# Query sums of squares in a dilated-attention layer: three plain float32 products on three strips of columns in place of six products of split squares

## The chip, the cores and the metric

The kernel runs on one core of a Trainium2 chip. The metric is the device time of one execution in microseconds (us); the median of the runs is compared. The profile comes from one execution of its own.

## The reference, as far as it matters

A two-layer decoder trunk over 512 tokens of width 1024: layer 0 is a gated DeltaNet mixer and a SwiGLU feed-forward, layer 1 is dilated sliding-window attention and a SwiGLU feed-forward. The change lies in the attention of layer 1. It has three groups of eight heads with 64 features each; every head's queries and keys are RMS-normalised before the scores:

```python
def _rmsnorm(x, w):
    y = x * lax.rsqrt(jnp.mean(x * x, axis=-1, keepdims=True) + RMS_EPS)
    return y * w
...
qkv = (h @ w_in).reshape(b, s, 3, N_DIL_GROUPS, DIL_HEADS_PER_GROUP, DIL_HEAD_DIM)
q = _rmsnorm(qkv[:, :, 0], q_norm)
k = _rmsnorm(qkv[:, :, 1], k_norm)
```

The change concerns the sum of x * x over the 64 features of a query head, for all heads and tokens.

## The kernel before, in words

Activations lie with features on the 128 partitions and the 512 tokens in the columns of a tile. A matrix product with weights is made of three products of halves: every operand is split into a rounded part and a remainder (type float32r), and high x high, high x low and low x high are summed in a PSUM bank (`gemm_steps`, line 431, product at line 441). ScalarE (ACT) rounds a weight block, VectorE (DVE) or GpSimd (POOL) subtracts to get the remainder. SyncE (SP) loads the weight blocks in the order of use (`stream`).

The order of the instructions of each engine is written when the program is built, by a planner (`Weave`): generators stand for jobs, `W.now` is the planned time of TensorE (PE), the wrapped engines `V` (DVE), `S` (ACT) and `G` (POOL) carry planned busy times, and a `yield` of an engine, an event or a pool (`Banks`) parks a generator until the planned time has come. On the chip each engine runs its instructions in that order and waits on semaphores.

In the attention layer (`dilated`, line 1075) a tile of 128 features holds two heads, so each of the three groups g has four pairs p. The main loop runs the jobs of `DJOBS` (line 37): `q21` is the query tile of group 2, pair 1, `k12` the key tile of group 1, pair 2, `u` and `v` jobs make values. Each q or k job is 24 products of 512 columns. The work behind it:

- `q_post` (line 1136): ACT scales the bank into the query tile, and `squares` (line 1125) takes the squares out of the bank on ACT, rounds them with a second pass of ACT and subtracts on POOL. Then the bank and one page go back and the query is announced.
- `k_post` (line 1146): the same squares for a key tile, two products with a block matrix `bones` (lines 1156 and 1157), and a chain on ACT and DVE that scales the key tile itself. It is not changed but for the name of its operand.
- `factors` (line 1246), once for each pair p, when its three queries are there: six products (line 1256) with 6 columns of `bones` each put the sums of three groups x two heads into partitions 0 to 5 of one bank, each group's high and low squares added up. ACT copies the 6 x 512 sums, four turns (`turn`, line 1265) bring the tokens to the partitions, and a chain of small DVE operations makes the scale of the queries (`rq`) and the slopes (`sd`), without which the scores of the pair can't be masked.
- `near`, `far` and `value` (lines 1320, 1373, 1421) make scores, exponentials and outputs of a pair. Scores are plain float32 products (`mat`, line 422) of 64 partitions, the two heads one after the other in the code.

`mat` counts max(2n, n + m) x 0.833 ns of PE for n columns, 0.853 us for 512. Pages are buffers of 128 x 512 floats, 59 of them, of which the planner gives the attention's jobs 30 (`pages`); a q job asks for four, a k job for five (line 1240). `dconst` (line 1060) loads the constants and rounds `bones` during the first feed-forward layer. In the first layer a blocked triangular solve (`merge`) uses plain products of 32x32 on strips of the array; in its second step three products run over each block, the first and the third from partitions 0 to 31 into partitions 32 to 63 and 0 to 31 of the bank, the second from 64 to 95 into 64 to 95.

Of the kernel before, what the change touches and what calls it, by code (L numbers as in the profile page):

```python
# [12 lines left out]
F32R = mybir.dt.float32r  # L13
I32 = mybir.dt.int32
AF = mybir.ActivationFunctionType
OP = mybir.AluOpType
# [6 lines left out]
NCH = T // 128  # L23
# [149 lines left out]
class Trunk:  # L173
# [248 lines left out]
    def mat(self, out, lhsT, rhs, start=True, stop=True):  # L422
        self.nc.tensor.matmul(out, lhsT=lhsT, rhs=rhs, start=start, stop=stop)  # L423
        n, m = math.prod(rhs.shape[1:]), lhsT.shape[-1]
        self.weave.now += max(2 * n, n + m) * 0.833e-3

    def turn(self, out, in_, ident=None):
        self.nc.tensor.transpose(out, in_, self.ident if ident is None else ident)  # L428
        self.weave.now += 0.107
# [630 lines left out]
    def dconst(self):  # L1060

        nc, V = self.nc, self.V
        late = self.ctx.enter_context(self.tc.tile_pool(name="late", bufs=1))
        tile = lambda n, name, dtype=F32: late.tile([128, n], dtype, name=name)
        dc = tile(512 + 96 + 146 + 2 + 36, "dc")
        nc.sync.dma_start(dc, self.a["dconsts"])
        dist = [dc[:, 0:256], dc[:, 256:384], dc[:, 384:512]]
        slopes = lambda p: dc[:, 512 + p * 24:512 + (p + 1) * 24].rearrange("p (g c h) -> p g c h", g=3, c=NCH)
        bones, wqk, eps = tile(146, "bones", F32R), tile(1, "wqk"), tile(1, "eps")
        V.tensor_copy(bones, dc[:, 608:754])  # L1070
        V.scalar_tensor_tensor(wqk, dc[:, 754:755], -0.0625, dc[:, 755:756], op0=OP.mult, op1=OP.mult)
        V.memset(eps, EPS)
        self.dc = dist, slopes, bones, wqk, eps, dc[:, 756:788], dc[:, 788:792]

    def dilated(self):

# [2 lines left out]
        mat, turn = self.mat, self.turn  # L1079
        W, V, S, G, sm, chain, main = self.weave, self.V, self.S, self.G, self.sm, self.ch, self.main  # L1080
        AX = mybir.AxisListType.X
        HB = NCH * 2
        ch = lambda c: slice(c * 128, (c + 1) * 128)
        seg = lambda t: t.rearrange("p (r n) -> p r n", r=4)
        mixed = lambda t, g: t if g else t.rearrange("p (r b n) -> p b r n", b=4, r=4)
        plain = lambda t, g: t if g else t.rearrange("p (b r n) -> p b r n", b=4, r=4)
        with tc.tile_pool(name="ak", bufs=1) as ak, tc.tile_pool(name="aw", bufs=2) as aw:
            dist, slopes, bones, wqk, eps, place, block = self.dc
            half = lambda h: slice(h * 64, (h + 1) * 64)
            fac = lambda i: rr[:, i].rearrange("p (g c) -> p g c", g=3)[:, :, :, None].to_broadcast([128, 3, NCH, 2])  # L1090
            rr = ak.tile([128, 3, 12], F32, name="rr")
# [20 lines left out]
            pages, scores, spaces, both = Banks(W, APAGES), Banks(W, SCORES), Banks(W, VALUES), Banks(W, 1)  # L1112
            qT, kT, vs, qs, rq, sd, om, pt, os_, done, gm = ({} for _ in range(11))
# [8 lines left out]
                done[key] = done.get(key, 0) + 1  # L1122
                return done[key] == n

            def squares(x, out=lambda t: t):

                sq, sh, sl = self.page(), self.page(F32R), self.page(F32R)
                S.activation(out(sq), x, AF.Square)
                yield S
                S.activation(sh, sq, AF.Copy)  # L1130
                yield S
                G.tensor_sub(sl, sq, sh.bitcast(F32))
                yield G
                return sq, sh, sl

            def q_post(g, p, ps):
                q = self.page()
                S.activation(plain(q, g), mixed(ps, g), AF.Copy, scale=wqk)
                sq, sh, sl = yield from squares(mixed(ps, g), lambda t: plain(t, g))
                main.release(0.0)  # L1140
                pages.release(0.0)
                qT[g, p] = q
                qs[g, p] = sh, sl
                W.fire(("q", g, p), G)

            def k_post(g, p, ps):
                t = self.page()
                yield "rb", 2
                V.tensor_mul(plain(t, g), mixed(ps, g), mixed(self.rb, g))
                main.release(V)  # L1150
                yield V
                sq, sh, sl = yield from squares(t)
                y = self.page()
                yield sm
                pn = self.bank()
                self.nc.tensor.matmul(pn, lhsT=bones[:, :128], rhs=sh, start=True, stop=False)
                self.nc.tensor.matmul(pn, lhsT=bones[:, :128], rhs=sl, start=False, stop=True)
                W.now += 0.427
                pages.release(0.0)
                pages.release(0.0)  # L1160
                S.activation(y, pn, AF.Ln, bias=eps)
                S.activation(y, y, AF.Exp, scale=-0.5)
                S.activation(sq, y, AF.Square)
                yield S
                V.scalar_tensor_tensor(sq, pn, EPS, sq, op0=OP.add, op1=OP.mult)
                sm.release(V)
                yield V
                V.scalar_tensor_tensor(y, sq, -3.0, y, op0=OP.add, op1=OP.mult)
                yield V
                pages.release(0.0)  # L1170
                V.tensor_mul(t, t, y)
                pages.release(V)
                kT[g, p] = t
                W.fire(("k", g, p), V)
# [62 lines left out]
            def job(names):  # L1237
                posts = []
                for j in names:
                    post, n = {"q": (q_post, 4), "k": (k_post, 5)}[j[0]]  # L1240
                    for _ in range(n):
                        yield pages
                    posts.append(lambda ps, f=post, g=int(j[1]), p=int(j[2]): f(g, p, ps))
                yield from self.together(posts, 2)

            def factors(p):


                yield ("orders",)
                for g in range(3):  # L1250
                    yield "q", g, p
                yield sm
                t = self.bank()
                for g in range(3):
                    for i, s in enumerate(qs[g, p]):
                        self.nc.tensor.matmul(t[:6], lhsT=bones[:, 128 + g * 6:134 + g * 6], rhs=s,  # L1256
                                              start=g + i == 0, stop=g + i == 3)
                        W.now += 0.2134
                        pages.release(0.0)
                yield pages  # L1260
                sums = self.page()[:6]
                S.activation(sums, t[:6], AF.Copy)
                yield S
                for c in range(NCH):
                    turn(t[:, c * 6:c * 6 + 6], sums[:, ch(c)], self.ident[:6, :6])
                pages.release(0.0)
                x = aw.tile([128, 3, NCH, 2], F32, name="fx", bufs=3)
                y = aw.tile([128, 3, NCH, 2], F32, name="fy", bufs=3)
                f = lambda t: t.rearrange("p g c h -> p (g c h)")
                V.tensor_mul(x, t[:, :24].rearrange("p (c g h) -> p g c h", c=NCH, g=3), fac(1))  # L1270
                sm.release(V)
                yield V
                V.tensor_scalar(f(x), f(x), EPS, None, op0=OP.add)
                yield V
                yield from self.rsqrt(f(y), f(x), aw)
                yield V
                V.tensor_mul(x, x, y)
                rq[p] = aw.tile([128, 3, NCH, 2], F32, name="rq", bufs=4)
                V.tensor_mul(rq[p], y, fac(0))
                yield V  # L1280
                V.tensor_mul(x, x, fac(2))
                yield V
                sd[p] = aw.tile([128, 3, NCH, 2], F32, name="sd", bufs=4)
                V.tensor_mul(sd[p], x, slopes(p))
                W.fire(("rq", p), V)
# [343 lines left out]
def layout(i):  # L1629
    i = {k: np.asarray(v) for k, v in i.items()}  # L1630
    a = {}
    x = i["x"][0]
# [24 lines left out]
    p = np.arange(128)  # L1657
# [7 lines left out]
    q = p % 32 * 4 + p // 32  # L1665
    d = q[:, None] - q[None, :]
    d0 = np.concatenate([np.where(d <= 0, d + 128, far), np.where(d >= 0, d, far)], axis=1)
    d = p[:, None] - p[None, :]
    d1 = np.where(d >= 0, 4 * d, far)
# [2 lines left out]
    slopes = [np.broadcast_to(-(2.0 ** (-8.0 * (head(pair) + 1) / 24)), (3, NCH, 2)).reshape(-1) for pair in range(4)]  # L1672
    slopes = np.broadcast_to(np.concatenate(slopes), (128, 96))
    same = (p[:, None] // 64 == p[None, :] // 64) / 64.0
    which = [np.where(np.arange(6) // 2 == g, p[:, None] // 64 == np.arange(6) % 2, 0) for g in range(3)]
    table = np.concatenate([d0, d1, d2, slopes, same] + which, axis=1).astype(np.float32)
    place = p[:, None] % 32 == np.arange(32)[None, :]
    block = p[:, None] // 32 == np.arange(4)[None, :]
    places = np.concatenate([place, block], axis=1).astype(np.float32)
# [18 lines left out]
```

## Time and profile before

| | us |
|---|---|
| median of 3 runs | 1392.67 |
| lowest and highest run | 1391.41, 1393.38 |
| profiled execution | 1394.09 |
| its span, first to last instruction | 1392.3 |

The profile's engines: PE is matmul, PEld the weight load that overlaps it, DVE VectorE, ACT ScalarE, POOL GpSimd. Idle time of an engine that is not the bottleneck costs nothing. Nearly all vector and scalar instructions carry line 83, that of the wrapper; they are told apart by tile names (`page`, `bank`, `wl`, `pp`, `fx`). A plain float32 product shows as two matmul records, a product of halves as one.

### The profile page before, as it was taken

How to read it: one execution, taken by the hardware profiler on the slowest of the kernel's cores; microseconds unless marked ns; L12 is line 12 of the kernel's file. 1: busy time of each engine (PE TensorE's matmuls, PEld its weight loads, DVE VectorE, ACT ScalarE, POOL GpSimd, SP SyncE). 2: the span in 40 equal slices, each digit the busy share in tenths (PEclk: the TensorE clock that was granted, in tenths of full speed). 3: DMA queues.
4: the chain of work that ended last, by engine and by line, in shares of the span. 5: the costliest groups of instructions: out<-in, count | busy, mean ns of one | idle time of the engine just before them, and what ended most of it. 6: DMA issues, size and time to landing. Idle time of an engine off the chain costs nothing.

```text
span 1392.3 us, 18305 instructions
## 1 busy us (share of the span) xinstructions
PE 1358.0 (98%) x7040; PEld 1121.7 (81%) x7040; DVE 811.9 (58%) x1476; ACT 591.9 (43%) x1268; POOL 265.8 (19%) x234
## 2 busy tenths in 40 slices
PE   8899989999999999999999999999989999999998
PEld 5688878878888888888888888889768888888887
DVE  7888766777555455434437456897675555554222
ACT  4654556863333333322246444665533333332221
POOL 5533800124111111111212111100141111110000
PEclk9999999999999999999999999999999999999999
DMA  4224240134233333333232332111123332333331
GB/s 161 63 74 121 76 119 20 31 122 127 82 101 96 95 102 91 99 98 96 86 91 91 93 90 63 60 46 47 39 67 107 92 105 91 95 103 104 110 107 57
DMA packets 48328, 122.52 MB, mean 88 GB/s; under 512 B 16624, under 2 KB 17008, under 8 KB 48240
## 3 DMA queue, kind: packets, MB, share of 16 engines
q1 hardware_dynamic: 47952, 121.21, 29.0%
q8 instruction: 55, 0.90, 0.3%
q14 instruction: 33, 0.27, 0.1%
q10 hardware_dynamic: 288, 0.14, 0.0%
HBM read 117.66 MB, written 3.67 MB: 87 GB/s over the span
## 4 chain that ended last, share of the span: by engine, by line
PE 84%; DVE 7%; ACT 3%; POOL 3%; issue 2%; DMA 1%; SPq 0%; DVEq 0%; ACTq 0%; POOLq 0%
PE bank L441 71%; PE bank L423 7%; DVE page L83 4%; PE bank L1192 3%; PE bank L428 2%; POOL xblk L83 2%; POOL tblk L83 1%; ACT page L83 1%; DVE wl L83 1%; ACT pp L83 1%; DMA wraw<-in_w 0%; ACT wh L83 0%; PE bank L1256 0%; DVE rsqrt L83 0%; DVE pp L83 0%
## 5 line engine op out<-in xcount | busy, mean ns | idle before, releaser
L441 PE MATMUL bank<-page,wh 128*128 128x512 f32 x2912 | 950.6, 395 | 9.3 <-DVE page L83 4.6
L441 PEld LDWEIGHTS bank<-page,wh 128*128 128x128 f32 x2912 | 550.0, 190 | 128.6 <-DVE page L83 6.5
L441 PE MATMUL bank<-page,wl 128*128 128x512 f32 x1632 | 645.1, 395 | 2.5 <-DVE wl L83 2.4
L83 ACT ACTIVATE wh<-wraw 128x512 fp32r<-128x512 f32 (+1 forms) x432 | 256.3, 616 | 468.6 <-PE bank L441 261.2
L83 DVE TENSOR_TENSOR wl<-wraw,wh 128x512 fp32r<-128x512 f32 (+1 forms) x408 | 341.3, 856 | 162.3 <-ACT wh L83 161.9
L441 PEld LDWEIGHTS bank<-page,wl 128*128 128x128 f32 x1632 | 309.4, 190 | 67.3 <-DVE wl L83 5.2
L83 POOL TENSOR_TENSOR page<-page 128x512 f32<-128x512 f32 (+2 forms) x122 | 179.0, 1470 | 923.0 <-DVE page L83 559.4
L83 DVE TENSOR_TENSOR page<-bank,page 128x512 f32<-128x512 f32 (+1 forms) x123 | 84.7, 690 | 228.8 <-PE bank L441 216.9
L83 ACT ACTIVATE page<-page 128x512 f32<-128x512 f32 (+2 forms) x224 | 140.4, 629 | 123.1 <-POOL page L83 65.9
L441 PE MATMUL bank<-hl,wh 128*128 128x512 f32 x352 | 139.0, 395 | 0.0
L441 PEld LDWEIGHTS bank<-hl,wh 128*128 128x128 f32 x352 | 66.1, 188 | 14.0
L83 DVE TENSOR_TENSOR page<-page,bank 128x512 f32<-128x512 f32 x40 | 27.4, 686 | 71.1 <-PE bank L441 63.9
L83 ACT ACTIVATE pp<-pp,om,rq 128x128 f32<-128x128 f32 (+1 forms) x96 | 43.1, 509 | 13.4 <-DVE om L83 13.2
L1192 PE MATMUL bank<-wh,page 128*128 128x256 f32 x256 | 48.3, 288 | 0.0
L83 DVE SCALAR_TENSOR_TENSOR page<-bank,cp,page 128x511 f32<-128x511 f32 (+2 forms) x63 | 46.7, 742 | 1.6 <-ACT page L83 1.0
L83 DVE SCALAR_TENSOR_TENSOR page<-page,cp 128x512 fp32r<-128x512 f32 (+3 forms) x39 | 45.0, 1166 | 3.7 <-ACT page L83 3.7
L83 DVE SCALAR_TENSOR_TENSOR page<-page 128x512 f32<-128x512 f32 (+1 forms) x52 | 41.8, 804 | 1.1 <-ACT page L83 0.3
L83 POOL TENSOR_TENSOR wl<-wraw,wh 128x512 fp32r<-128x512 f32 x24 | 33.2, 1388 | 45.4 <-ACT wh L83 45.3
L1192 PEld LDWEIGHTS bank<-wh,page 128*128 128x128 f32 x256 | 39.9, 191 | 1.8 <-issue 1.0
L83 ACT ACTIVATE page<-bank 128x512 f32<-128x512 f32 (+4 forms) x37 | 21.0, 568 | 42.1 <-PE bank L423 28.7
L83 DVE SCALAR_TENSOR_TENSOR pp<-dc,sd,bank 128x128 f32<-128x128 f32 (+1 forms) x96 | 33.5, 372 | 8.5 <-PE bank L423 8.5
L1192 PE MATMUL bank<-wl,page 128*128 128x256 f32 x128 | 36.4, 284 | 1.0 <-DVE wl L83 0.9
(174 smaller groups left out, 916.6 us busy)
## 6 DMA issues: line engine op xcount, KB each, us to landing
wraw<-in_fin SPq DMA_DIRECT2D x88, 512.0 KB, 3.6
wraw<-in_w SPq DMA_DIRECT2D x32, 512.0 KB, 3.6
wraw<-in_fout SPq DMA_DIRECT2D x32, 448.0 KB, 3.3
wraw<-in_dqk SPq DMA_DIRECT2D x24, 512.0 KB, 3.6
wraw<-in_fout SPq DMA_DIRECT2D x16, 512.0 KB, 3.6
wraw<-in_w0o SPq DMA_DIRECT2D x8, 512.0 KB, 3.6
wraw<-in_dv SPq DMA_DIRECT2D x8, 512.0 KB, 3.6
page<-in_x SPq DMA_DIRECT2D x8, 256.0 KB, 6.6
```

The source lines that it names most:

```text
L83: return f(out, *args, **kw)
L423: self.nc.tensor.matmul(out, lhsT=lhsT, rhs=rhs, start=start, stop=stop)
L428: self.nc.tensor.transpose(out, in_, self.ident if ident is None else ident)
L441: self.nc.tensor.matmul(ps, lhsT=lhsT[:, c], rhs=rhs, start=k + i == 0, stop=k == len(xs) - 1 and i == 2)
L1192: self.nc.tensor.matmul(ps[c], lhsT=x[:, ch(c)], rhs=w[:, k * 256:(k + 1) * 256], start=b + k + t == 0, stop=b == 1 and k == 3 and t == 2)
```

## The change

The squares of the queries are no longer split. For each pair, three plain float32 products, one for each group, with one 128 x 32 matrix `which` (columns 0 and 1 pick the two heads, the others are zero) write partitions 0 to 31, 32 to 63 and 64 to 95 of one bank. The planner counts the three as one. The copy takes 96 partitions, the turns 96 x 96 of the identity, and the sums are read from two of every 32 columns. `bones` keeps its 128 columns for the keys; `which` stays unrounded in the constants.

```diff
@@ dconst @@
-        dc = tile(512 + 96 + 146 + 2 + 36, "dc")
+        dc = tile(512 + 96 + 160 + 2 + 36, "dc")
...
-        bones, wqk, eps = tile(146, "bones", F32R), tile(1, "wqk"), tile(1, "eps")
-        V.tensor_copy(bones, dc[:, 608:754])
+        bones, wqk, eps = tile(128, "bones", F32R), tile(1, "wqk"), tile(1, "eps")
+        V.tensor_copy(bones, dc[:, 608:736])
...
-        self.dc = dist, slopes, bones, wqk, eps, dc[:, 756:788], dc[:, 788:792]
+        self.dc = dist, slopes, bones, dc[:, 736:768], wqk, eps, dc[:, 770:802], dc[:, 802:806]
@@ q_post @@
-                sq, sh, sl = yield from squares(mixed(ps, g), lambda t: plain(t, g))
-                main.release(0.0)
-                pages.release(0.0)
+                qs[g, p] = self.page()
+                S.activation(plain(qs[g, p], g), mixed(ps, g), AF.Square)
+                main.release(S)
                 qT[g, p] = q
-                qs[g, p] = sh, sl
-                W.fire(("q", g, p), G)
+                W.fire(("q", g, p), S)
+                yield S
@@ job @@
-                    post, n = {"q": (q_post, 4), "k": (k_post, 5)}[j[0]]
+                    post, n = {"q": (q_post, 2), "k": (k_post, 5)}[j[0]]
@@ factors @@
                 for g in range(3):
-                    for i, s in enumerate(qs[g, p]):
-                        self.nc.tensor.matmul(t[:6], lhsT=bones[:, 128 + g * 6:134 + g * 6], rhs=s,
-                                              start=g + i == 0, stop=g + i == 3)
-                        W.now += 0.2134
-                        pages.release(0.0)
+                    mat(t[g * 32:g * 32 + 32], which, qs[g, p])
+                    pages.release(0.0)
+                W.now -= 2 * 0.853
                 yield pages
-                sums = self.page()[:6]
-                S.activation(sums, t[:6], AF.Copy)
+                sums = self.page()[:96]
+                S.activation(sums, t[:96], AF.Copy)
                 yield S
                 for c in range(NCH):
-                    turn(t[:, c * 6:c * 6 + 6], sums[:, ch(c)], self.ident[:6, :6])
+                    turn(t[:, c * 96:c * 96 + 96], sums[:, ch(c)], self.ident[:96, :96])
...
-                V.tensor_mul(x, t[:, :24].rearrange("p (c g h) -> p g c h", c=NCH, g=3), fac(1))
+                V.tensor_mul(x, t[:, :384].rearrange("p (c g h) -> p g c h", c=NCH, g=3)[:, :, :, :2], fac(1))
@@ layout @@
-    which = [np.where(np.arange(6) // 2 == g, p[:, None] // 64 == np.arange(6) % 2, 0) for g in range(3)]
-    table = np.concatenate([d0, d1, d2, slopes, same] + which, axis=1).astype(np.float32)
+    which = p[:, None] // 64 == np.arange(32)
+    table = np.concatenate([d0, d1, d2, slopes, same, which], axis=1).astype(np.float32)
```

## Rows read from the trace of the kernel before

**Rows 1.** The page's head: busy us (share of the span) xinstructions.

```profile
PE 1358.0 (98%) x7040; PEld 1121.7 (81%) x7040; DVE 811.9 (58%) x1476; ACT 591.9 (43%) x1268; POOL 265.8 (19%) x234
```

**Rows 2.** Stretches: us, busy PE, PEld, DVE, ACT, POOL (xinstructions), granted clock, DMA.

```profile
820.00:840.00 20.00, 19.41 (x133) 16.38 (x132) 13.49 (x37) 9.63 (x18) 2.92 (x2) 1.00 0.20 57
...
940.00:960.00 20.00, 18.98 (x164) 18.04 (x164) 17.69 (x47) 15.71 (x35) 0.00 (x0) 1.00 0.14 38
...
980.00:1000.00 20.00, 16.99 (x111) 13.83 (x109) 10.65 (x18) 11.18 (x23) 0.00 (x0) 0.99 0.17 53
1000.00:1006.00 6.00, 6.00 (x14) 4.40 (x15) 3.51 (x6) 3.10 (x5) 2.92 (x3) 0.50 0.00 0
...
1028.00:1034.00 6.00, 6.00 (x15) 4.69 (x16) 1.11 (x2) 0.00 (x0) 0.00 (x0) 0.53 0.14 55
```

**Rows 3.** The chain that ended last, 755 to 800 us: start, us, piece.

```profile
771.03 1.39 PE bank L1256 x6
...
773.55 0.34 PE bank L428 x4
...
780.99 0.44 PE bank L428 x4
```

**Rows 4.** Groups of ACT and POOL, 700 to 930 us: count | busy us, mean ns | idle before.

```profile
L83 ACT ACTIVATE page<-page 128x512 fp32r<-128x512 f32 x25 | 15.5, 624 | 0.3
...
L83 POOL TENSOR_TENSOR page<-page 128x512 fp32r<-128x512 f32 x24 | 32.2, 1343 | 177.4 <-ACT page L83 156.8 <-issue 10.9 <-DVE page L83 6.8
```

**Rows 5.** Timeline of PE around the scores at 864 us: start, us, instruction.

```profile
864.04 0.39 PE L441 MATMUL bank<-page,wl 128*128 128x512 f32 x1
864.27 0.39 PE L441 MATMUL bank<-page,wh 128*128 128x512 f32 x1
864.59 1.16 PE L423 MATMUL bank<-page 64*128 64x128 f32 x16
865.68 0.50 PE L441 MATMUL bank<-page,wh 128*128 128x512 f32 x1
```

**Rows 6.** The chain that ended last, end of the attention stage.

```profile
964.43 5.94 PE bank L423 x54
...
981.38 1.54 ACT pp L83 x4
```

**Rows 7.** Timeline of PE in the first layer's solve, second step.

```profile
192.88 0.19 PE L423 MATMUL bank<-MX,xblk 32*32 32x32 f32 x1
192.88 0.20 PE L423 MATMUL bank<-xblk,MX 32*32 32x32 f32 x2
192.91 0.19 PE L423 MATMUL bank<-MX,xblk 32*32 32x32 f32 x1
192.91 0.20 PE L423 MATMUL bank<-xblk,MX 32*32 32x32 f32 x2
```

**Rows 8.** Timeline of all engines before the first scores, 823 to 827 us.

```profile
823.23 0.69 DVE L83 SCALAR_TENSOR_TENSOR page<-page 128x512 f32<-128x512 f32 x1
...
824.58 1.29 POOL L83 TENSOR_TENSOR page<-page 128x512 fp32r<-128x512 f32 x1 [6.18 <-ACT page L83]
824.62 1.79 DVE L83 TENSOR_TENSOR page<-page 128x512 f32<-128x512 f32 x1
...
826.57 0.38 PE L423 MATMUL bank<-page 64*128 64x128 f32 x2 [0.59 <-DVE page L83]
```

**Rows 9.** Timeline of DVE between 862 and 904 us.

```profile
872.35 0.93 DVE L83 TENSOR_SCALAR fx<-fx 128x24 f32<-128x24 f32 x1
...
874.33 0.16 DVE L83 TENSOR_SCALAR fy<-fx 128x24 int32<-128x24 int32 x1
...
880.14 0.35 DVE L83 SCALAR_TENSOR_TENSOR pp<-dc,sd,bank 128x128 f32<-128x128 f32 x1 [1.81 <-PE bank L423]
```

**Rows 10.** Who waited for whom, PE alone, 700 to 978 us: us in total, times, longest.

```profile
PE bank L1192 <- DVE wl L83: 0.9, 1, 0.9
PE bank L423 <- DVE page L83: 0.7, 2, 0.6
```

More of the change, by code (lines that the diff above doesn't have):

```diff
@@ L1068, in dconst @@
         slopes = lambda p: dc[:, 512 + p * 24:512 + (p + 1) * 24].rearrange("p (g c h) -> p g c h", g=3, c=NCH)
-        bones, wqk, eps = tile(146, "bones", F32R), tile(1, "wqk"), tile(1, "eps")
-        V.tensor_copy(bones, dc[:, 608:754])
-        V.scalar_tensor_tensor(wqk, dc[:, 754:755], -0.0625, dc[:, 755:756], op0=OP.mult, op1=OP.mult)
+        bones, wqk, eps = tile(128, "bones", F32R), tile(1, "wqk"), tile(1, "eps")
+        V.tensor_copy(bones, dc[:, 608:736])
+        V.scalar_tensor_tensor(wqk, dc[:, 768:769], -0.0625, dc[:, 769:770], op0=OP.mult, op1=OP.mult)
         V.memset(eps, EPS)
-        self.dc = dist, slopes, bones, wqk, eps, dc[:, 756:788], dc[:, 788:792]
+        self.dc = dist, slopes, bones, dc[:, 736:768], wqk, eps, dc[:, 770:802], dc[:, 802:806]
     def dilated(self):
@@ L1087, in dilated @@
         with tc.tile_pool(name="ak", bufs=1) as ak, tc.tile_pool(name="aw", bufs=2) as aw:
-            dist, slopes, bones, wqk, eps, place, block = self.dc
+            dist, slopes, bones, which, wqk, eps, place, block = self.dc
             half = lambda h: slice(h * 64, (h + 1) * 64)
@@ L1123, in finished, with squares @@
                 return done[key] == n
-            def squares(x, out=lambda t: t):
+            def squares(x):
                 sq, sh, sl = self.page(), self.page(F32R), self.page(F32R)
-                S.activation(out(sq), x, AF.Square)
+                S.activation(sq, x, AF.Square)
                 yield S
@@ L1155, in k_post @@
                 pn = self.bank()
-                self.nc.tensor.matmul(pn, lhsT=bones[:, :128], rhs=sh, start=True, stop=False)
-                self.nc.tensor.matmul(pn, lhsT=bones[:, :128], rhs=sl, start=False, stop=True)
+                self.nc.tensor.matmul(pn, lhsT=bones, rhs=sh, start=True, stop=False)
+                self.nc.tensor.matmul(pn, lhsT=bones, rhs=sl, start=False, stop=True)
                 W.now += 0.427
```

## The prediction

> **What bounds the kernel now.** I read the page's head first: TensorE (PE) is busy for 98% of the span [rows 1], so a step is worth what it takes from PE's queue, or what it takes from a wait that PE ends on. The table of stretches comes next [rows 2]: in the attention stage the clock is granted whole and PE is full. It idles 0.59 us in 820 to 840, 1.02 us in 940 to 960 and 3.01 us in 980 to 1000; after 1000 come two stretches of 6 us at half clock. VectorE (DVE) is busy 17.69 us of 20 in 940 to 960, so it is the next engine. The chain of waits then tells whether the changed products lie on the path: the six split products of one pair of heads stand on it with 1.39 us, with their four turns behind them [rows 3]. There are four such groups, at 771, 828, 868 and 910 us, all on the chain. Last I read the groups of ScalarE (ACT) and GpSimd (POOL) [rows 4].
>
> A measurement of this kernel can tell about 0.2% from no change, 2.8 us. The profiled execution took 1394.09 us (span 1392.3 us and 1.8 us around it), 1.4 us above the median of 1392.67 us; I sum against 1394.09 and move the difference to the median.
>
> **The products.** Removed: 24 split products, 4 x 1.39 = 5.6 us of PE [rows 3]. Added: 12 plain float32 products with 512 columns. The trace has none of that width. A plain product shows as two records, and one of 128 columns takes 5.94 / 54 = 0.11 us [rows 6]; four times the columns make 0.44 us a record, 0.88 us a product.
>
> Do three run at once? The nearest rows are the 32x32 products of the first layer's solve [rows 7]: three strips, two of them fed from the same rows of the array with different data. Their records come as one and two, one and two, a new triple after 0.03 us, as long as a single record of 32 columns would take by rows 6 (0.11 / 4). So strips of columns that share rows run together, and first halves stand beside first halves. Then a group takes 2 x 0.44 = 0.88 us and what it costs to enter and leave strips. For that I take the scores, two strips of rows [rows 5]: 16 records, eight steps of 0.11 = 0.88 us, and yet 1.09 us pass until the next product starts, 0.21 us of rim; and the product before them holds 0.32 us where its neighbours hold 0.23, another 0.09. The stationary operand here has 32 columns and not 128, so its load should show less. I take 1.10 us a group, between 0.88 (no rim) and 1.18 (all of it). Saved: 0.29 x 4 = 1.2 us. The outer bound is no overlap: 6 x 0.44 + 0.30 = 2.94 us, 1.55 us more a group.
>
> One thing speaks against two steps. If the two records of a product are issued one behind the other and no record overtakes, a strip's second half holds up the next strip's first, and the group is a staircase of four steps, 4 x 0.44 + 0.30 = 2.06 us, 0.67 more than now. The records of rows 7 interleave and show no staircase, so I sum with two steps and keep four as a rival. The Trainium skill (TensorE: Matmul & The Clock Gate, Part 3, "Packing small matmuls") has a rule that would give the staircase: matmuls start and end strictly in program order, without reordering. By it the sum below would be +2.5 us and not -1.4; the trace agrees with it only if the order issued is already the interleaved one, which no row here shows.
>
> **The turns.** Before: four turns of 6 rows in 0.34 us. After: four of 96 rows and 96 columns. The nearest rows are full 128x128 turns, 0.44 us for four [rows 3]; I take that end, +0.10 a group, +0.4 us. The other end is no change. The weighted read of the turned sums has 24 elements as before, and the copy out of the bank has 512 columns as before: nothing.
>
> **ScalarE and GpSimd.** Twelve of the 25 rounding copies go, 12 x 0.624 = 7.5 us of ACT, and twelve of the 24 subtractions, 12 x 1.343 = 16.1 us of POOL [rows 4]. PE's work covers both, and the cover stays: the waits of PE between 700 and 978 us are three on DVE's tiles and weights, none on a bank [rows 10]. So I cost the work itself at nothing, also the earlier return of the query's bank and the two pages fewer.
>
> What it does to DVE counts. At 824.58 POOL subtracts a query's halves (by its place in the order of jobs those of q01), and beside it DVE's product of the key tile takes 1.79 us, where the DVE operations just before it, on as many columns, take 0.69. PE waits 0.59 us for that tile [rows 8]. With the subtraction gone the product ends about 1.1 us earlier, and then PE's own work is late next: -0.6 us. Bounds: 0 (the order shifts and something else is beside it) to -0.6.
>
> The same slowing shows in the busy stretch: 0.93 us at 872 on a tile of 24 columns where the next such operation takes 0.16 [rows 9]. But DVE then waits for PE itself, 1.81 us before 880.14 [rows 9], so this relief is swallowed and I cost it at nothing. The idle time in 940 to 960 is mostly a wait on DVE's split of weights, 0.9 us [rows 10]; little of the relief reaches it. Bounds: 0 to -1.0.
>
> **What moves.** The program's order comes from a planner. It now sees a query ready about one copy and one subtraction earlier (0.62 + 1.34 = 2 us), releases the bank earlier, counts 0.853 us of PE a group where it counted six of 0.2134 = 1.28, and asks for two pages a query, not four. So factors, scores and what follows are placed earlier among the weight products. No DMA is added; SP's queue keeps its order, and the constants' load grows by 14 columns and is issued a whole feed-forward layer earlier. That reordering has no row. I bound it by the waits that stand there: it can remove the 1.02 us of 940 to 960, or add a wait of that kind.
>
> Sum: -1.2 + 0.4 - 0.6 = -1.4 us: 1392.7 for the profiled execution, 1391.3 for the median.
>
> **The rivals.**
> *More waits go.* As forecast, and also the waits in 940 to 960 (-1.0) and half of one stretch at half clock. A product there takes 0.43 us (6 us with 14 records [rows 2]) where it takes 0.23 [rows 5], so a stretch costs 14 x 0.2 = 2.8 us, half of it 1.4. Together -3.8 us, 1388.9. For it: the last pair's factors come 2 us earlier and the tail is a chain of latencies. Against: DVE is nearly full there, and the stretches come after a tail that hangs on the last exponentials [rows 6], whose work does not change.
>
> *The strips don't run together.* The change then doesn't do what it says: +1.55 x 4 + 0.4 - 0.6 = +6.0 us, 1398.7. For it: no row has three strips over all 128 rows with 512 columns. Against: rows 7. It decides from a group of about 2.1 us upward (1.39 + (2.8 + 0.2) / 4).
>
> *Staircase.* The strips overlap by one half only, four steps as worked out above: +0.67 x 4 + 0.4 - 0.6 = +2.5 us, 1395.2. For it: the three products wait for three tiles of their own, and the code issues each product whole. Against: the solve's products are issued whole too, and interleave [rows 7].
>
> *A new wait at the end of the stage.* The order shifts so that scores or values of the last pair stand ahead of something that is not ready; PE is in order, so all weight products behind them wait. One such wait has the size of the 0.9 us on the weights [rows 10], and the time at half clock grows with it by up to a stretch, 2.8 us: -1.4 + 0.9 + 2.8 = +2.3; with two such waits +3.2 us, 1395.9, which I take. It decides beyond 4.2 us of new waits and lost clock (2.8 + 1.4).
>
> **How the numbers follow.** Forecast 0.50, more waits gone 0.23, new wait 0.13, strips apart 0.07, staircase 0.07. Faster by over 0.2%: nearly all of the second case and a little of the first, 0.26. Slower: strips apart, most of the new wait and a little of the staircase, 0.18. Within: 0.56. The forecast's own range is 1390.0 to 1392.3 (below: groups of 0.88 us and turns at nothing, -2.0 - 0.6; above: groups of 1.18 us and the wait at 826 kept, -0.8 + 0.4). The whole range reaches below to a whole stretch at half clock gained beside the waits of the second case (-1.4 - 1.0 - 2.8, 1387.5), above a little beyond the new wait (1396.5), and leaves out the strips apart.
>
> **What would show it.** Three products a pair as six records of about 0.44 us in two steps; from the first of them to the next product's start 1.0 to 1.2 us, and not 2 or 3. Turns of about 0.44 us for four. POOL with 12 subtractions, ACT with 13 rounding copies. The key tile's product before the first scores (near 825 us) at 0.7 us and PE without a wait there. Idle time between 940 and 1000 and the two half-clock stretches as before. The prediction is wrong if the group holds PE for over 1.4 us, or if idle time before 1000 us or time at half clock moves by more than 2 us either way.

## The result, and the profile after

The changed kernel took 1400.47 us (median of 4 runs, 1399.77 to 1402.10) beside 1392.96 us before (4 runs, 1391.41 to 1393.38): 1.0058 times the time, 95% interval 1.0046 to 1.0070, so 7.5 us slower. The prediction said 1391.3 us in a range of 1387.5 to 1396.5: wrong, and on the wrong side. The profiled execution took 1402.1 us with a span of 1400.1; its head on the page, beside [rows 1]:

```profile
span 1400.1 us, 18258 instructions
PE 1360.6 (97%) x7040; PEld 1122.7 (80%) x7040; DVE 805.8 (58%) x1476; ACT 584.7 (42%) x1256; POOL 250.4 (18%) x222
```

POOL has 12 subtractions fewer and ACT 12 rounding copies fewer, but PE is busy for 2.6 us longer. Yet the edited operations are not what costs the time. The timeline of PE at the first group of the changed kernel (start, us, instruction):

```profile
770.60 0.39 PE L441 MATMUL bank<-page,wh 128*128 128x512 f32 x1
770.92 1.06 PE L423 MATMUL bank<-page,dc 128*32 128x512 f32 x6
771.91 0.50 PE L441 MATMUL bank<-page,wh 128*128 128x512 f32 x1
772.24 0.39 PE L441 MATMUL bank<-page,wl 128*128 128x512 f32 x1
...
772.94 0.39 PE L441 MATMUL bank<-page,wl 128*128 128x512 f32 x1
773.17 0.49 PE L428 MATMUL bank<-cc,page 96*128 96x96 f32 x4
773.45 0.71 PE L441 MATMUL bank<-page,wh 128*128 128x512 f32 x2
```

and in the kernel before, behind its group and around its turns:

```profile
772.26 0.39 PE L441 MATMUL bank<-page,wl 128*128 128x512 f32 x1
772.49 0.61 PE L441 MATMUL bank<-page,wh 128*128 128x512 f32 x2
...
773.17 0.39 PE L441 MATMUL bank<-page,wh 128*128 128x512 f32 x1
773.49 0.41 PE L428 MATMUL bank<-cc,page 6*128 6x6 f32 x4
```

From the first record of the group to the next product 0.99 us pass, and the product before holds PE for 0.32 where others hold it for 0.23: 1.08 us where [rows 3] had 1.39. The product behind the group holds 0.33 (771.91 to 772.24), which the kernel before did not have (772.26 to 772.49, 0.23); with it a group costs 1.19 us, 0.2 less than before. The four turns take 0.28 us where they took 0.34, and the product ahead of them holds 0.23 where it held 0.32. So it is in the first and third groups; in the other two, next to scores, the turns take 0.42 and 0.39 us. The groups of ACT and POOL from 700 to 930 us, beside [rows 4]:

```profile
L83 ACT ACTIVATE page<-page 128x512 fp32r<-128x512 f32 x13 | 8.1, 622 | 0.2
...
L83 POOL TENSOR_TENSOR page<-page 128x512 fp32r<-128x512 f32 x12 | 16.3, 1360 | 195.9 <-ACT page L83 190.0 <-issue 5.8
```

The loss stands in two other places. One is the end of the attention stage: who waited for whom, PE alone, 700 to 1020 us (total, times, longest):

```profile
PE bank L441 <- ACT page L83: 5.6, 1, 5.6
PE bank L441 <- DVE page L83: 2.3, 1, 2.3
PE bank L1192 <- DVE wl L83: 0.4, 2, 0.2
PE bank L1192 <- ACT wh L83: 0.4, 1, 0.4
```

In the kernel before, the longest wait of that table was

```profile
PE bank L441 <- ACT page L83: 2.6, 2, 2.3
```

The stretches that answer to [rows 2]:

```profile
820.00:840.00 20.00, 19.41 (x120) 15.36 (x119) 11.86 (x37) 7.80 (x14) 0.99 (x1) 1.00 0.27 80
940.00:960.00 20.00, 19.93 (x172) 18.39 (x170) 16.07 (x44) 15.40 (x36) 0.00 (x0) 1.00 0.16 53
...
980.00:1000.00 20.00, 17.55 (x118) 15.51 (x117) 6.67 (x11) 11.15 (x25) 0.00 (x0) 0.91 0.16 53
1000.00:1020.00 20.00, 14.39 (x51) 11.04 (x50) 14.19 (x17) 7.45 (x12) 7.92 (x6) 0.83 0.09 27
...
600.00:696.00 96.00, 96.00 (x417) 78.03 (x416) 39.22 (x51) 24.97 (x44) 16.61 (x12) 1.00 0.33 96
```

The waits of [rows 10] on a page of 0.6 and on weights of 0.9 us are gone or smaller; but before, the two longest waits up to 1020 us were 2.3 and 0.9 us, now they are 5.6 and 2.3, and behind the one of 2.3 the granted clock falls, 0.91 over 980 to 1000 where it was 0.99.

The other place is the last row: 600 to 696 us is the first feed-forward layer, whose code the change doesn't touch, at full clock without a gap, and PE does 417 products there. Before, in the same stretch:

```profile
600.00:696.00 96.00, 96.00 (x421) 78.61 (x420) 41.65 (x52) 25.61 (x45) 19.11 (x13) 1.00 0.32 95
```

Three output products (`hl,wh`, `page,wl`, `page,wh`) take 693.3 ns after and 686.7 before, in both feed-forward layers; the gate and up products take 680.0 in both kernels. There are 352 such triples: 6.6 ns x 352 = 2.3 us. What differs is an address: with 18 columns less in `bones` and 14 more in `dc` (4 columns, 16 bytes, in sum, and rounding in the layout) everything laid out behind the constants lies 32 bytes lower, the moving operand `hl` among it: 172928 where it was 172960.

### The profile page after: what moved, and what is told of

It is laid out like the page before. It is cut to its first block, busy times and chain, and to the rows that moved or that the text cites. A ratio compares the mean times of both kernels' runs of the same rounds, so it can differ in the third digit from the quotient of the medians.

```text
span 1400.1 us, 18258 instructions
## 1 busy us (share of the span) xinstructions
PE 1360.6 (97%) x7040; PEld 1122.7 (80%) x7040; DVE 805.8 (58%) x1476; ACT 584.7 (42%) x1256; POOL 250.4 (18%) x222
## 4 chain that ended last, share of the span: by engine, by line
PE 84%; DVE 6%; POOL 3%; ACT 3%; issue 2%; DMA 1%; SPq 1%; DVEq 0%; ACTq 0%; POOLq 0%
PE bank L441 71%; PE bank L423 8%; DVE page L83 4%; PE bank L1192 3%; PE bank L428 2%; POOL xblk L83 2%; POOL tblk L83 1%; ACT page L83 1%; DVE wl L83 1%; DMA wraw<-in_w 1%; ACT wh L83 0%; SPq L759 0%; ACT pp L83 0%; DVE rsqrt L83 0%; ACT junk L83 0%
## 5 line engine op out<-in xcount | busy, mean ns | idle before, releaser
L441 PE MATMUL bank<-page,wh 128*128 128x512 f32 x2912 | 955.5, 397 | 16.3 <-DVE page L83 6.9
L441 PEld LDWEIGHTS bank<-page,wh 128*128 128x128 f32 x2912 | 551.2, 190 | 134.9 <-DVE page L83 8.8
L441 PE MATMUL bank<-page,wl 128*128 128x512 f32 x1632 | 646.7, 396 | 2.5 <-DVE wl L83 2.4
L441 PEld LDWEIGHTS bank<-page,wl 128*128 128x128 f32 x1632 | 310.2, 190 | 71.3 <-DVE wl L83 5.2
L83 POOL TENSOR_TENSOR page<-page 128x512 f32<-128x512 f32 (+2 forms) x110 | 163.1, 1485 | 944.7 <-DVE page L83 555.0
L83 ACT ACTIVATE page<-page 128x512 f32<-128x512 f32 (+2 forms) x212 | 133.2, 629 | 122.7 <-POOL page L83 65.9
L441 PE MATMUL bank<-hl,wh 128*128 128x512 f32 x352 | 138.3, 393 | 0.0
L441 PEld LDWEIGHTS bank<-hl,wh 128*128 128x128 f32 x352 | 65.9, 187 | 14.5
```

What stands on the lines that cost most here:

```text
L83: return f(out, *args, **kw)
L441: self.nc.tensor.matmul(ps, lhsT=lhsT[:, c], rhs=rhs, start=k + i == 0, stop=k == len(xs) - 1 and i == 2)
```

## The experiments

**Which part costs what (e1 to e3).** e1 gives the changed kernel its old addresses:

```diff
-        bones, wqk, eps = tile(128, "bones", F32R), tile(1, "wqk"), tile(1, "eps")
+        bones, wqk, eps = tile(136, "bones", F32R)[:, :128], tile(1, "wqk"), tile(1, "eps")
```

> The changed kernel with bones 8 columns wider, so that every tile behind it in memory, the halves hl of the feed-forward among them, lies where it lay before the change. Theory (part of the loss is the place of hl): the three products of an output block of the feed-forward take 0.687 us again and not 0.693, 352 times, -2.1 us, median about 1398.4; the tail of the attention stage stays as late as in the changed kernel. Rival (the slower pace is a matter of the run): pace 0.693 in some runs, median about 1400.5.

Measured: 1397.04 us (ratio 1.0033, 1.0021 to 1.0046); three output products take 686.7 ns again. The address is worth 3.4 us of medians, 2.3 of them by the pace; the rest is within the spread of the runs, and no run shows a cause for it. The waits at the end are still there, 5.6 us on ACT's page and 2.3 on DVE's.

e2 is e1 with the planner told the old story: copies and subtractions are counted but not issued, a group counts 6 x 0.2134 us, four pages are asked for. The order of each engine is that of before, without the removed instructions.

```diff
                 S.activation(plain(qs[g, p], g), mixed(ps, g), AF.Square)
+                yield S
+                S.count(q, q)
+                yield S
+                G.count(q, q, q)
+                yield G
...
-                    mat(t[g * 32:g * 32 + 32], which, qs[g, p])
-                    pages.release(0.0)
-                W.now -= 2 * 0.853
+                    self.nc.tensor.matmul(t[g * 32:g * 32 + 32], lhsT=which, rhs=qs[g, p], start=True, stop=True)
+                    for _ in range(2):
+                        W.now += 0.2134
+                        pages.release(0.0)
```

> The changed kernel with the wider bones of the run before, and the planner told the old story: it counts the twelve copies and subtractions that are no longer there, 0.2134 us for each of six products, and four pages a query, so that all engines keep the order of the kernel before, less what the change removed. Theory (the loss is the new order at the end of the attention stage): the saving of products, turns and the wait before the first scores shows, about -2 us against before, 1390.5 to 1391.5, and the time at half clock is as before. Rival (the new products, or what waits for them, cost the time whatever the order): 1397 to 1399.

Measured: 1391.47 us beside 1392.64 (ratio 0.9990, 0.9981 to 0.9999). So the instructions themselves save 1.2 us, and the order alone is e1 - e2 = 5.6 us.

e3 is the reverse, the instructions of before in the order of after:

```diff
-                sq, sh, sl = yield from squares(mixed(ps, g), lambda t: plain(t, g))
-                main.release(0.0)
-                pages.release(0.0)
+                sq, sh, sl = self.page(), self.page(F32R), self.page(F32R)
+                S.activation(plain(sq, g), mixed(ps, g), AF.Square)
+                self.nc.scalar.activation(sh, sq, AF.Copy)
+                self.nc.gpsimd.tensor_sub(sl, sq, sh.bitcast(F32))
+                main.release(S)
```

> The kernel before with its split squares, copies, subtractions and six products, but in the order that the planner gave the changed kernel (copies and subtractions not counted, queries announced after the squares, 0.853 us a group, two pages a query). Theory (the order costs it): the tail gets late and the half clock long as in the changed kernel, 1396 to 1399. Rival (the order is harmless, the new products cost): 1392 to 1394.

Measured: 1401.11 us (ratio 1.0062, 1.0049 to 1.0074), with the same waits at the end, 2.3 and 5.6 us. Here the order costs 8.5 us, more than the 5.6 between e1 and e2, in part since the groups now also stand ahead of subtractions that are not done (1.6 us of waits on POOL's pages and 0.5 on ACT's).

**What happens at the end (e1, e2, e5).** PE's timeline at the end of the attention stage in the changed kernel. `cc,pp` are the turns of probabilities, `pp,v` the values, L441 here the output products, which the planner uses as filler:

```profile
980.13 1.25 PE L428 MATMUL bank<-cc,pp 128*128 128x128 f32 x10
...
982.60 0.60 PE L428 MATMUL bank<-cc,pp 128*128 128x128 f32 x4
983.32 0.50 PE L441 MATMUL bank<-page,wh 128*128 128x512 f32 x1
986.15 0.80 PE L441 MATMUL bank<-page,wh 128*128 128x512 f32 x1 [2.33 <-DVE page L83]
...
988.46 0.92 PE L441 MATMUL bank<-page,wh 128*128 128x512 f32 x2
989.21 0.39 PE L441 MATMUL bank<-page,wl 128*128 128x512 f32 x1
989.44 0.60 PE L428 MATMUL bank<-cc,pp 128*128 128x128 f32 x4
...
993.49 5.97 PE L423 MATMUL bank<-pp,v 128*128 128x128 f32 x52
...
1006.44 1.52 PE L441 MATMUL bank<-page,wh 128*128 128x512 f32 x2 [5.61 <-ACT page L83]
```

and the work of DVE ahead of that first wait:

```profile
982.78 0.69 DVE L83 TENSOR_TENSOR wl<-wraw,wh 128x512 fp32r<-128x512 f32 x1 [0.39 <-ACT wh L83]
984.21 1.29 DVE L83 TENSOR_TENSOR wl<-wraw,wh 128x512 fp32r<-128x512 f32 x2 [0.73 <-ACT wh L83]
985.42 0.68 DVE L83 TENSOR_TENSOR page<-page 128x512 fp32r<-128x512 f32 x1
```

An output product needs the remainder of an earlier pair's output, the last row. That subtraction stands on DVE behind splits of weights, which wait for ACT, where the roundings of these weights stand among exponentials (one of 0.49 us at 983.17, eleven in 4.76 us from 984.59). PE is in order, so the last pair's turns and values queue behind the product; and the eight products from 986.15 to 989.44 take 3.3 us, 1.5 more than at the 0.23 us of [rows 5], because the clock has fallen after the wait. The same place in e2:

```profile
979.13 2.55 PE L428 MATMUL bank<-cc,pp 128*128 128x128 f32 x11
981.95 0.50 PE L441 MATMUL bank<-page,wh 128*128 128x512 f32 x1 [0.28 <-ACT page L83]
982.45 0.93 PE L428 MATMUL bank<-cc,pp 128*128 128x128 f32 x4
...
995.52 0.39 PE L441 MATMUL bank<-page,wl 128*128 128x512 f32 x1
998.23 0.51 PE L441 MATMUL bank<-page,wh 128*128 128x512 f32 x1 [2.33 <-ACT page L83]
```

From the traces of e1 and e2, counted from the same product at about 711 us: the last exponential ends at 275.8 and 275.1 us, the last turn starts at 279.3 and 275.5, the last value product at 286.5 and 282.3, the last wait ends at 293.1 and 287.4. So e1 is 0.7 us late at the exponentials, loses 3.1 us up to the last turn (wait, low clock, products ahead of the turns), 0.4 up to the values, and 1.4 behind them, where the two heads' chains come together and not staggered (DVE takes the steps of both heads as pairs of 1.41 us in e1, one by one in 0.69 us in e2): 5.6 us, the whole difference. Of the output products, 24 lie between last score and last value in e1 and 3 behind it, 16 and 11 in e2; that is why the last wait is long: the filler has been used up. (In e5 below 14 stand behind it, 11 more; 11 x 0.23 = 2.5 us, and the last wait is 2.5 us shorter.)

e5 moves only PE's order at this place; DVE, ACT and POOL keep e1's order:

```diff
-                    W.fire(("out", p), V)
+                    W.fire(("out", p), V.ready() + W.latency + (3.0 if p == 2 else 0.0))
```

> The kernel of e1 (changed kernel, old addresses), but the planner is told that the output of the last pair but one is ready 3 us later. Only TensorE's order differs, and only at the end of the attention stage: the turns of the last pair's probabilities (16 in a row) stand ahead of the output products, not behind the product that waited 2.34 us. My theory (the waiting product holds the turns and the values behind it, and the products used up there are missing before the last wait): the wait of 2.3 us on a DVE page goes, PE waits for ScalarE's exponentials instead (they run until about 987.6 us in e1), the last turns come about 3 us earlier, the last wait shrinks from 5.6 to about 3.5 us, time 1394.0 to 1395.0 (e1: 1397.0; e2: 1391.5). Not all of the 5.6 us between e1 and e2 can come back, since the two heads' outputs still come together. Rival (the exponentials or the chain behind the values set the end, and the wait is only where it shows): 1396.5 to 1397.5.

Measured: 1395.64 us (9 runs, 1391.38 to 1397.46; ratio 1.0017, 1.0004 to 1.0029), 1.4 below e1, less than I expected and more than the rival allowed. The runs spread widely and the intervals of e1 and e5 overlap, so the size of the gain is uncertain; the waits of the profiled run say more:

```profile
PE bank L441 <- ACT page L83: 3.1, 1, 3.1
PE bank L428 <- ACT pp L83: 2.7, 2, 2.0
```

The wait on DVE's page has gone and the last wait has shrunk by 2.5 us, but PE now waits 2.7 us for the exponentials, the clock falls behind that wait too (0.50 over 984 to 988 us), and the heads' chains still come together. So the product that stood in the way was a part of the loss. The rest goes with the order of the tail as a whole (e1 against e2); which piece of that order costs how much is not shown.

**What the planner was told (e6, e9, e10).** Two inputs of the planner changed: when a query is announced and its bank returned, and what a group counts. All three kernels issue e1's instructions; only their order differs.

```diff
-                W.now -= 2 * 0.853
+                W.now += 1.07 - 3 * 0.853
```

> The kernel of e1, but the planner counts the three products of a group with 1.07 us (as long as the trace of the changed kernel shows them) and not 0.853. Theory A (the planner places the tail badly because it thinks PE further ahead than it is: a number that is too small): order and time come back towards e2, 1391.5 to 1393. Theory B (the end of the stage turns on chance: any small shift of the planner's times gives another order, good or bad, and a truer number does not protect): anything between 1391 and 1398; a wait of over 2 us at 980 to 990 us stands or not as the order of that run decides. Theory C (the earlier announcement of the queries does the harm): 1396 to 1398.

```diff
-                W.now -= 2 * 0.853
+                W.now += 6 * 0.2134 - 3 * 0.853
```

> The kernel of e1, but the planner counts a group's products with the old 1.28 us; the queries are announced early, as in the changed kernel. In the written order 22 of the last pair's turns stand with only eight output products between them, and the values of the two heads begin one after the other, as in e2. Theory (the time follows the written order of the tail, whatever input of the planner made it): the two heads' last chains come staggered, the last wait is near 2.3 us, 1390.5 to 1393.0. Rival (the early announcement of the queries costs the time): 1396 to 1398, as e1.

e10 has the late announcement of e2's diff (with its `S.count` and `G.count`), but the new count and two pages.

> The kernel of e1, but the planner announces the queries, and gives the bank back, as late as before, when a rounding copy and a subtraction would have ended; a group's products are counted with 0.853 us, as in the changed kernel. In the written order only twelve turns stand ahead of the first values of the last pair and the two heads' values begin one after the other. Theory (the time follows the order of the tail): 1390.5 to 1393.0, a last wait near 2.3 us. Rival (the small count costs the time): 1396 to 1398, as e1. With e1, e2 and e9 this makes all four pairs of the two inputs.

| median us | group counts 0.853 | 1.07 | 1.28 |
|---|---|---|---|
| announced early | 1397.04 (e1) | 1397.79 (e6) | 1393.10 (e9) |
| announced late | 1386.37 (e10) | | 1391.47 (e2) |

The ratios to before are 1.0038 (1.0024 to 1.0052) for e6, 0.9994 (0.9986 to 1.0003) for e9 and 0.9949 (0.9935 to 0.9963) for e10. Neither input is to blame alone: the new count costs 3.9 us with the early announcement and gains 5.1 with the late one. (e2 asks for four pages a query and e10 for two, but with e2's other inputs the planner writes the same order for either number.) The late announcement was the faster one with either count, by 10.7 us with the new one and by 1.6, within the noise, with the old one. A count as long as the measured 1.07 us doesn't help. The same instructions take from 1386 to 1398 us by their order. e6's own time fits its theories B and C alike; e9, announced early and as fast as before, speaks against C as the whole reason, and e10 falls below the range of B. Five plans show that the order decides, and not a rule for the planner. e10 came out 4 us below what I expected, the best of the five:

```profile
PE bank L441 <- ACT page L83: 1.4, 1, 1.4
PE bank L441 <- DVE wl L83: 1.0, 1, 1.0
PE bank L441 <- DVE page L83: 0.2, 1, 0.2
```

(975 to 1020 us.) Its timeline shows what goes with it:

```profile
976.34 0.49 PE L428 MATMUL bank<-cc,pp 128*128 128x128 f32 x3
976.58 0.48 PE L1196 MATMUL bank<-wh,page 128*128 128x256 f32 x2
...
977.37 0.93 PE L428 MATMUL bank<-cc,pp 128*128 128x128 f32 x7
978.06 0.48 PE L1196 MATMUL bank<-wh,page 128*128 128x256 f32 x2
...
996.05 0.50 PE L441 MATMUL bank<-page,wh 128*128 128x512 f32 x1 [1.42 <-ACT page L83]
```

Products of the value projection (L1196) stand between the turns while the exponentials come in, so PE doesn't wait there; at the granted clock of 1.00 the last wait ends at 283.0 us of the stage, 4.4 before e2's. No run changed these products alone, so that they are the reason is my reading.

**Where hl lies (e4, e7, e8, e11).** One unused tile ahead of `hl` in both feed-forward layers, in e2's kernel (e4), in the kernel before (e7) and in e10 (e11); e8 has other widths (8 columns in the first layer, 496 in the second):

```diff
             gs, hs = {}, {}
+            fp.tile([128, 480], F32, name="gap")
```

> The kernel of old order, and in both feed-forwards a gap of 480 columns ahead of hl, so that hl lies at the same place within 2048 bytes as the pages. Theory (the pace of a product of halves hangs on where hl lies against the pages): three products take 0.680 us as with pages alone, 352 x 7 ns = -2.5 us against the kernel of old order, about 1388.5. Rival (hl is slow for another reason, as its distance from the weights): no change against the kernel of old order.

> The kernel before, with one unused tile of 480 columns ahead of the remainder tile hl in both feed-forward layers: hl then lies 800 bytes past a multiple of 2048, as the pages do, and not 928. Nothing else differs. Theory (the pace of the output products hangs on where hl lies): 680 ns for three products in place of 687, 352 triples, 2.5 us less: 1390.2. Rival (the gain of e4 came from its missing pages and products): 687 ns and 1392.7.

> The kernel before with hl at 960 bytes past a multiple of 2048 in the first feed-forward layer (gap of 8 columns) and at 864 in the second (gap of 496). Known so far: 800 gives 680 ns for three products, 896 gives 693, 928 gives 687. If only the same offset as the pages' is good, both layers show 687 or more; if the pace follows the distance to the pages' offset, 864 shows less than 687 and 960 more; if it follows whether the offset is a multiple of 64, 960 gives 693 and 864 gives 680 to 687. Time within 3 us of 1392.7 in all cases.

> The kernel of e10 with the unused tile of e4 and e7 ahead of hl in both feed-forward layers; the order of every engine is that of e10. If the gain of hl's place adds up with the gain of the order: 680 ns for three products in place of 687, 352 triples, 2.4 us less than e10's 1386.4, so 1384.0 (within a run's spread 1382.5 to 1385.5). If the shorter feed-forward shifts the clock's low stretches against it: 1386.

| hl, bytes past a multiple of 2048 | ns for three output products | kernels |
|---|---|---|
| 800, as the pages and wh | 680.0 | e4, e7, e11 |
| 864 | 696.0 | e8, second layer |
| 896 | 693.3 | after |
| 928 | 686.7 | before, e1, e2 |
| 960 | 696.7 | e8, first layer |

e4 took 1388.75 us (ratio 0.9974, 0.9962 to 0.9985), 2.7 below e2. e7 took 1390.51 (0.9987, 0.9978 to 0.9996), 2.2 below before, as the pace says (6.7 ns x 352 = 2.4). Its stretch of the first feed-forward layer (PE alone: busy, instructions, granted clock, DMA) has 425 products where before had 421 and after 417:

```profile
600.00:696.00 96.00, 96.00 (x425) 1.00 0.33 96
```

e8 refutes two of the rules I had offered: 864 is slower than 928, and neither the distance to the pages' offset nor a multiple of 64 orders the values. The full pace was seen at the pages' own offset alone; no offset beyond these five was tried, so whether that is the condition stays open. Its one run of 1399.49 us is outside the 3 us expected: against the profiled run of before 3.4 us of its 5.4 go to the slower products (10.0 and 9.3 ns x 176) and 2.4 to stretches ahead of the first feed-forward layer, in code that is the same (0.4 come back elsewhere); for the latter I have no cause, but e7's profiled run lost 1.7 us in the same stretches and e7 is the faster kernel.

e11 took 1385.56 us (4 runs, 1381.10 to 1387.28; ratio 0.9938, 0.9916 to 0.9961). The pace is 680.0 ns, but only 0.8 us of the 2.4 shows against e10, whose interval overlaps: in the profiled run 1.9 us were lost between 924 and 1032 us, with the clock at 0.62 from 996 to 1000 where e10 had it whole. It is the fastest kernel of the study, 7.3 us below the 1392.88 us of the kernel before that were measured beside it; e4, e7, e10 and e11 all beat both kernels.

**What the strips are worth (e12).** e10 with a group's three products in one strip, added up there, so that it leaves out the separate sums of the three groups:

```diff
-                    mat(t[g * 32:g * 32 + 32], which, qs[g, p])
+                    mat(t[:32], which, qs[g, p], start=g == 0, stop=g == 2)
```

> The kernel of e10, but a group's three products go to one strip (partitions 0 to 31 of the bank, one sum over the three groups), and copy and turns take 32 partitions; the sums are then not kept apart by group. Measures what the strips of columns are worth by themselves. If one product alone takes two records of 0.22 us (a column of a plain product at the pace of a product of halves), a group takes 1.33 us and more, and strips save 0.3 us a group; if a record takes 0.44 us, as the prediction has it, a group takes 2.65 us and strips save 1.6 us a group, 6.4 us in all, so 1392 to 1393 in place of 1386.4. Turns of 32 columns: 0.28 us for four if the 96 columns cost nothing, less if the width counts.

```profile
771.95 2.76 PE L423 MATMUL bank<-page,dc 128*32 128x512 f32 x6
774.64 0.50 PE L441 MATMUL bank<-page,wl 128*128 128x512 f32 x1
...
775.99 0.43 PE L428 MATMUL bank<-cc,page 32*128 32x32 f32 x4
776.35 0.49 PE L441 MATMUL bank<-page,wh 128*128 128x512 f32 x1
```

2.69 us where the strips take 0.99, 1.7 us a group, and 1395.59 us in one run, 9.2 above e10's median. Between the two traces 1.9 us a group are lost (7.6 in all, slower turns included), and the rest at the end of the stage. The record of 0.43 us that the prediction scaled up from 128 columns is right; with 0.09 us ahead and 0.11 behind, as with the strips, the group costs 2.89 us, so without the strips the change would lose 1.5 us a group against the split products.

## Why the prediction was wrong

**The products: right in the mechanism, the saving smaller.** Forecast 1.10 us a group in two steps of 0.44, saved 1.2 us. Counted as the forecast counted it, from the rim ahead to the next product, a group takes 1.08 us; the sum left out that the product behind holds 0.10 us more too, as [rows 5] had it behind the scores (the product at 865.68 holds PE for 0.33). With it 1.19 us, saved 0.2 a group, some 0.85 in all. The two rivals about the strips are out: e12 shows what no overlap would look like, and a staircase would have taken 2.06 us. In the trace the first halves start at 770.918, 770.925 and 770.932, the second at 771.372, 771.379 and 771.385. The rule of the Trainium skill that I had set against it (TensorE: Matmul & The Clock Gate, Part 3, "Packing small matmuls": products start and end in program order) agrees with these starts, product by product; what falls is my reading of it, that a second half would hold up the next strip.

**The turns: mis-sized, with the wrong sign.** Forecast 0.44 us for four and +0.4 in all; measured 0.28 us in two of the four groups, with no rim on the way in, where turns of 6 rows held 0.34 and 0.09 on the way in (32 rows in e12: 0.36 and 0.09). In the other two groups, next to scores, it comes out even. That makes some -0.35 in e2. The 0.44 us of [rows 3] for full turns was the length of a piece of the chain; on PE's timeline those turns, at 780.83, hold PE for 0.35 us with no rim on the way in, so the same trace already had them cheaper than those of 6 rows. The error here is larger than that of the products and of the other sign: groups and turns together save 0.36, 0.26, 0.36 and 0.25 us in e2's trace, 1.2 in all, where the sum had 0.8.

**ScalarE and GpSimd: right in the cause.** The key tile's product takes 0.69 us in e2 and 0.68 after, where [rows 8] had 1.79. In e2 the wait is gone and 820 to 840 is full:

```profile
820.00:840.00 20.00, 20.00 (x140) 1.00 0.18 57
```

In the changed kernel the new order puts other waits there, 0.36 and 0.22 us on weights at 833, and the stretch is as idle as before. With the order of before the working holds: -1.2 for groups and turns and -0.6 make -1.8, and from 760 us to the last turns e2's trace gains 1.9 us on that of before; the medians give -1.2 (interval -2.6 to -0.1).

**What moves: the step that failed.** "It can remove the 1.02 us of 940 to 960, or add a wait of that kind" bounded a new order of the whole stage by waits of the old one, and the forecast then took it at nothing. Both came: 940 to 960 went from 1.02 us idle to 0.07, and the new order of the tail brought a wait of 2.3 us, 1.5 us at low clock behind it and a last wait longer by 3.3, of which 5.6 us reach the end (e1 against e2). The rival "A new wait at the end of the stage" had the place, the in-order queue and the low clock right. Its price, 4.6 us (two waits of 0.9 and a stretch of 2.8), lies 1.0 below the measured one: the wait was one, and longer, and the grown last wait was not in it. e1's 1397.0 lies 1.1 above the rival's 1395.9. What was wrong was to take the new order at nothing and give the new wait a chance of 0.13: of e1, e6 and e9, three plans with the early announcement, two lose 4 to 5 us and one comes out as before. Three plans are few, but the old order's time was not a safe thing to assume.

**A term that was missing.** The wider constants and narrower `bones` were costed at nothing. They moved `hl` by 32 bytes, 2.3 us by the pace, and that took the time from the edge of the range to well outside. The sum from the runs: -1.2 (instructions) + 5.6 (order) + 3.4 (addresses, of which 2.3 are explained) = +7.8, beside +7.5 measured. The terms are steps from one kernel to the next, so they must add up but for the spread of the medians; the sum is no second proof. That the order and the addresses each cost is shown by e2 and e3, and by e1, e4 and e7.

## What to carry to other kernels

Where a planner writes the order, an edit has two prices, that of its instructions and that of the order that it tips; measure them apart by keeping the old counts in the planner while the instructions go, and try several orders before judging an edit. Here the edit is worth -1.2 us in the old order and +4.4 in the one it came with; in the best order found the changed kernel is 6.9 us below before, but the instructions of before were not tried in that order, so how much of it the edit itself gives is not shown. And when a tile's size changes, compare the addresses of everything laid out behind it: a kernel's untouched part can run at another pace.

## What the runs showed of the hardware

- The pace of products of halves depends on where the moving operand lies: 680 to 697 ns for three, over five offsets of one tile, at full clock, with nothing else changed (e7 against before; table above).
- Three plain products with 128 rows, 512 columns and 32 stationary columns, in three strips of columns, run in little more than the time of one (0.88 us in e12): 0.99 us against 2.69 in one strip. One plain product takes 2 x 0.43 us, 3.8 times a product of halves at 0.227. The Trainium skill (FP8 and Floating Point Precision, TensorE Precision Notes) counts four passes for full float32, and the trace agrees.
- Between products of halves, turns of 96 rows cost less than turns of 32 or 6 rows: 0.28 us for four against 0.36 and 0.34, and the product ahead of them holds 0.23 us and not 0.32. Next to scores the advantage is gone (0.42 us).
- Behind the wait of 2.3 us that ends at 986.15 in the changed kernel the granted clock falls for some us: 0.71 over 984 to 988 and 0.87 over 988 to 992, between the whole clock (2.4 GHz) and half of it (1.2 GHz). The length of the last wait alone does not decide it: it is 1.42 us in e10 and in e11, which have one order, and behind it the clock is 1.00 over 996 to 1000 us in e10 and 0.62 in e11. The stretches at the low level differ between runs of one order: e2 gains 2.1 us on before between 997 and 1039 us, where both have the same order and the same last wait.
